# A token-mixer and MLP block with its mixers laid out in three stages: inputs, gates as Strassen sets, one output projection

## The chip, the core and the metric

The kernel runs on one core of a Trainium2 chip. Its time is the device time of one execution, in microseconds (us). The engines that matter are TensorE (PE, matrix products, with a queue of its own for loading weights, PEld), VectorE (DVE), ScalarE (ACT) and GpSimd (POOL). SyncE (SP) does nothing but issue the loads of weights; POOL issues most of the other DMAs. Matrices wait in the on-chip memory SBUF, products are summed in the banks of PSUM, and what does not fit is put in DRAM.

## The reference

One block works on 528 tokens (16 meta tokens and 512 of the sequence) of 2,048 channels, in float32. The first half is two token mixers with three gates, the second a squared-ReLU MLP.

```python
u = rmsnorm(h, norm1_g)                              # 528 x 2048
v_pool, v_lru, v_gelu, g_pool, g_lru = split(u @ w_in)   # five parts of 2048 columns
pool_out = pool_mixer(v_pool)      # causal window means over 2, 4, 8, 16 tokens, then a 512x512 map per group
xc = causal_depthwise_conv(v_lru)  # 4 taps
r, i = sigmoid(xc @ gate_a_w + gate_a_b), sigmoid(xc @ gate_x_w + gate_x_b)   # 8 heads of 256 channels
log_a = -8 * r * softplus(-lam);  a = exp(log_a);  bt = sqrt(-expm1(2 * log_a)) * i * xc
h_t = a_t * h_(t-1) + bt_t         # a scan over the tokens
lru_out = h_t * gelu(v_gelu)
merged = sigmoid(g_pool) * pool_out + sigmoid(g_lru) * lru_out
h = h + merged @ w_out             # 2048 x 2048
h = h + square(relu(rmsnorm(h, norm2_g) @ w1)) @ w2      # 2048 -> 8192 -> 2048
out = rmsnorm(h, final_g)          # the meta tokens are dropped
```

The three gates (g_lru, v_gelu, g_pool) and everything behind them are needed for the 512 tokens alone; v_lru and v_pool are needed for all 528, since the convolution, the scan and the windows look back.

## The kernel before

**Products.** Channels lie on the 128 partitions, tokens along the free axis; a matrix of 2,048 channels is 16 chunks. A weight chunk of 128 x 1024 is loaded from DRAM (SP's queue, 512 KB) and split in two: ACT copies it, rounded, to `whi` (L118), and DVE subtracts that from the chunk into `wlo` (L119). Data is split in the same way. Each product is then three matmuls, whi·xhi, whi·xlo and wlo·xhi (`mm3`, L353 and L635). `Weights` holds four raw chunks and four split ones and splits two ahead of the one in use: `W.next()` hands out a chunk, `W.advance()` asks for the splits of the next. So ACT and DVE split weights all the way through, in between the rest of their work. The order of an engine's instructions is set when the program is built: a scheduler interleaves the instructions of neighbouring steps, and each engine then works strictly through its row.

**Mixers (L308 to L606).** Four quarters of four chunks each. The list `jobs` gives their order: `VL` (a chunk of v_lru: 96 matmuls of 264 columns, then the convolution and the split of its result), `GA` (one LRU head: 48 matmuls of 264 columns, then tanh, reciprocal, sqrt and the scan), `GE`, `GL`, `GP` (one chunk of one gate: 48 matmuls of 512 columns), `VP` (v_pool, 96 matmuls of 264 columns, then window sums on POOL), `PW` (pool map), `WO` (a quarter of the output projection: for each of the 16 output chunks, 12 matmuls of 512 columns over the quarter's four merged chunks, added on DVE to the residual stream `ht`, L560). The first job, `V2`, makes two chunks of v_lru at once while x arrives. The operands x are split without the norm's factor; each evacuation from PSUM multiplies by `rstd` on DVE (`evac_full` L378, `evac` L383). `norm1` (job `N1`) makes `rstd` and stands between `GP` 0 and `GP` 1.

**MLP up (W1).** 32 Strassen sets. A set takes a 2 x 2 block problem (two output chunks by two token halves of 256, over two halves of the channels) and does it with seven products instead of eight: the operands `x11`, `t1`, `t2`, `x21`, `t3`, `x22`, `t4` are sums and differences of the four quarters of x. Each product is 8 chunks of 3 matmuls of 256 columns, 168 matmuls a set (`strassen`, L647; `mm3` L638). The weights' own sums are made on DVE (L107). `finish_h` (squares), `pre_scale`, `forms` (L272: residual times gain and a scale, L278, then the operands and their splits, L284 and L285) and the chain that makes `rho` (L616 to L633) prepare the operands while the last quarter of `WO` runs and behind it. Results of W1 are squared and put in DRAM (`y_sp`).

**MLP down (W2).** 38 steps of Strassen sets over a window of eight `slots` that POOL loads from DRAM, with sums added to `h_sp` in DRAM by DMA; then a last small product and the final norm.

## Time and profile before

| | |
|---|---|
| Times of three runs | 2546.42, 2546.8 and 2571.56 us; median 2546.8 us |
| Profiled execution | 2548.32 us, of which 2546.5 us lie between its first and last instruction (the span) |
| PE busy | 2472.1 us, 97% of the span |
| DVE busy | 1790.6 us, 70% |
| ACT busy | 1051.7 us, 41% |
| POOL busy | 255.0 us, 10% |
| Data read and written in DRAM | 280.85 MB and 54.13 MB |
| Mean granted clock of PE | 0.987 |

In time, the mixers reach to about 1196 us, then come W1 (to about 1859 us), W2 (to about 2460 us) and the tail. The chain of waits follows the work that ended last back to the start, each piece with its start and its length in us; where PE is named all along, PE is what the time goes by. The windows give each engine's busy time in a stretch, with the number of its instructions in brackets, the mean granted clock of PE as a part of full speed, the busy share of the DMA engines and the GB/s that they moved.

### The profile page before, as it was taken

The numbers are of one execution on the slowest core, as the hardware profiler recorded it, in microseconds if no ns is written. First come the engines' busy times: TensorE is split into PE (matmuls) and PEld (weight loads), VectorE is DVE, ScalarE is ACT, GpSimd is POOL, SyncE is SP. The second block draws the span as 40 slices with busy tenths as digits, with TensorE's granted clock in tenths as the row PEclk, the third lists the DMA queues.
The fourth block names the chain that finished last, engine by engine and source line by source line (L and its number), as shares of the span: only waits on it lengthen the run. The fifth ranks groups of instructions, "written<-read, shape, count | busy, mean of one in ns | idle before, by whom it ended". The sixth has DMA issues, their size and how long they took to land.

```text
span 2546.5 us, 41799 instructions
## 1 busy us (share of the span) xinstructions
PE 2472.1 (97%) x17558; PEld 2309.1 (91%) x17558; DVE 1790.6 (70%) x2120; ACT 1051.7 (41%) x1360; POOL 255.0 (10%) x258
## 2 busy tenths in 40 slices
PE   8999999999999999998599999999989999999997
PEld 7889898988889898986599999999979999999996
DVE  8834565445834456338988988988868888878778
ACT  5522233222422234224444444444545454545446
POOL 2100001100202002113100000000010000000010
PEclk9999999999999999999799999999989999999999
DMA  5233333332333323333354554555476665666553
GB/s 194 92 99 91 92 91 92 91 100 91 91 96 92 94 75 108 91 100 99 103 158 154 154 173 151 156 172 151 137 239 168 184 178 174 182 183 186 154 161 105
DMA packets 96604, 337.69 MB, mean 133 GB/s; under 512 B 10720, under 2 KB 18016, under 8 KB 96416
## 3 DMA queue, kind: packets, MB, share of 16 engines
q1 hardware_dynamic: 77648, 251.82, 32.9%
q0 software_dynamic: 18624, 83.11, 10.6%
q8 instruction: 137, 2.24, 0.4%
q14 instruction: 51, 0.42, 0.0%
q10 hardware_dynamic: 144, 0.10, 0.0%
HBM read 280.85 MB, written 54.13 MB: 132 GB/s over the span
## 4 chain that ended last, share of the span: by engine, by line
PE 90%; DVE 6%; issue 1%; DMA 1%; ACT 1%; POOL 0%; SPq 0%; DVEq 0%; ACTq 0%
PE ps_A L638 13%; PE ps_Ab L638 13%; PE ps_vp L357 7%; PE ps_gl L357 7%; PE ps_vl L357 7%; PE ps_B L638 7%; PE ps_gp L357 7%; PE ps_ge L357 7%; PE ps_Bb L638 6%; PE ps_wo L357 6%; PE ps_C L638 3%; PE ps_Cb L638 3%; PE ps_pw L357 2%; PE ga L357 2%; DVE wlo L119 1%
## 5 line engine op out<-in xcount | busy, mean ns | idle before, releaser
L118 ACT ACTIVATE whi<-raw 128x1024 fp32r<-128x1024 f32 (+5 forms) x423 | 428.4, 1015 | 803.1 <-issue 189.8
L119 DVE TENSOR_TENSOR wlo<-raw,whi 128x1024 fp32r<-128x1024 f32 (+5 forms) x423 | 510.2, 1208 | 221.1 <-ACT whi L118 216.2
L638 PE MATMUL ps_Ab<-slot,whi 128*128 128x256 f32 x1984 | 361.0, 283 | 8.4 <-ACT whi L118 3.0
L118 ACT ACTIVATE whi<-sum 128x1024 fp32r<-128x1024 f32 (+7 forms) x210 | 205.6, 979 | 343.8 <-DVE sum L107 165.9
L638 PEld LDWEIGHTS ps_Ab<-slot,whi 128*128 128x128 f32 x1984 | 307.0, 192 | 12.1 <-ACT whi L118 3.8
L638 PE MATMUL ps_Ab<-slot,wlo 128*128 128x256 f32 x992 | 280.3, 283 | 1.3 <-DVE wlo L119 1.2
L119 DVE TENSOR_TENSOR wlo<-sum,whi 128x1024 fp32r<-128x1024 f32 (+7 forms) x210 | 234.8, 1118 | 53.5 <-ACT whi L118 49.4
L638 PEld LDWEIGHTS ps_Ab<-slot,wlo 128*128 128x128 f32 x992 | 188.1, 190 | 2.4 <-DVE wlo L119 2.4
L638 PE MATMUL ps_Bb<-slot,whi 128*128 128x256 f32 x992 | 180.2, 282 | 1.6 <-ACT whi L118 1.6
L107 DVE TENSOR_TENSOR sum<-sum,raw 128x1024 f32<-128x1024 f32 (+7 forms) x140 | 156.5, 1118 | 4.7 <-DMA raw<-w 0.6
L638 PEld LDWEIGHTS ps_Bb<-slot,whi 128*128 128x128 f32 x992 | 152.9, 191 | 2.3 <-ACT whi L118 2.2
L638 PE MATMUL ps_Bb<-slot,wlo 128*128 128x256 f32 x496 | 139.7, 282 | 0.0
L357 PE MATMUL ps_vl<-uh,whi 128*128 128x264 f32 x512 | 106.2, 289 | 7.4 <-ACT whi L118 7.0
L357 PE MATMUL ps_vl<-ul,whi 128*128 128x264 f32 x512 | 105.4, 288 | 0.0
L357 PE MATMUL ps_vl<-uh,wlo 128*128 128x264 f32 x512 | 105.2, 287 | 0.0
L357 PE MATMUL ps_vp<-ul,whi 128*128 128x264 f32 x512 | 104.5, 285 | 0.0
L357 PE MATMUL ps_vp<-uh,wlo 128*128 128x264 f32 x512 | 104.3, 285 | 0.0
L357 PE MATMUL ps_vp<-uh,whi 128*128 128x264 f32 x512 | 104.2, 285 | 0.0
L357 PE MATMUL ps_ge<-ul,whi 128*128 128x512 f32 x256 | 101.2, 395 | 0.0
L357 PE MATMUL ps_gl<-ul,whi 128*128 128x512 f32 x256 | 101.2, 395 | 0.0
L357 PE MATMUL ps_gp<-ul,whi 128*128 128x512 f32 x256 | 101.2, 395 | 0.0
L357 PE MATMUL ps_gp<-uh,wlo 128*128 128x512 f32 x256 | 100.7, 393 | 0.0
(630 smaller groups left out, 6829.3 us busy)
## 6 DMA issues: line engine op xcount, KB each, us to landing
raw<-w SPq DMA_DIRECT2D x168, 512.0 KB, 4.2
raw<-w_in SPq DMA_DIRECT2D x159, 512.0 KB, 3.7
...
slot<-ysp POOLq DMA_DIRECT2D x31, 896.0 KB, 6.3
...
```

What stands on the lines that cost most here:

```text
L107: nc.vector.tensor_tensor(self.raw[o], self.raw[x], self.raw[y], op=ALU.add)
L118: nc.scalar.activation(hi[:, s], raw[:, s], AF.Copy)
L119: nc.vector.tensor_tensor(lo[:, s], raw[:, s], hi[:, s].bitcast(F32), op=ALU.subtract)
L357: PE.matmul(o, a, r, start=first and i == 0, stop=last and i == 2)
L638: PE.matmul(o, a, b, start=first and i == 0, stop=last and i == 2, skip_group_check=True)
```

## The change

The mixers are taken apart into three stages.

**Stage 1, inputs.** Only `VL`, `GA`, `VP`, `PW` and a new job `F` run, in a new written-out order. After `N1` a job `VR` makes chunks 0 and 1 of v_pool and, chunk by chunk ahead of its products, makes the operands of x anew with the norm's factor in them (`rescale_x`: DVE, ACT, DVE). From then on evacuations are plain copies on ACT. The chunks 0, 1 and 2 of v_lru, whose products were made with the old operands, still get the factor on DVE; their convolutions stand behind the rescaling. `F` makes Strassen operands of x for one pair of chunks: `t1` stays in SBUF, `t2`, `t3`, `t4` are put in DRAM (`f_sp`) and fetched at the stage's end (`fill`). Results of the scans and of the pool maps are put in DRAM (`lr_sp`, `pl_sp`). `F` also reads x from DRAM again, since the residual in SBUF gives up its place.

**Stage 2, gates.** For each of eight pairs of chunks, three Strassen sets (`gl`, `ge`, `gp`) of 168 matmuls of 256 columns. The elementwise work is done on tiles of 1,024 columns; the merged pair is split in two parts and put in DRAM (`m_sp`).

**Stage 3, output projection.** All merged chunks are in SBUF, and each output chunk sums over all 16 in PSUM (192 x 4 = 768 matmuls of 512 columns as before, without sums in `ht`): six output chunks at once for pairs 0 to 2, then pairs 3 to 6 one output chunk after another, and pair 7 in four quarters. Operands of W1 are made pair by pair meanwhile; four of the seven are put in DRAM (`g_sp`) and fetched as the merged chunks come free. The first W1 set begins with the first seven chunks of three products, and the last pair's operands are made behind that (`head`); `rho` is made in `middle`.

SBUF is laid out by hand in two large tiles, `a1` and `a2`, which the operands of all stages share. W1, W2 and the tail keep their work; their slots now lie in `a1` and `a2`, and x comes with its tokens ordered by halves. The new weight arrays `woa`, `wob`, `woc` are `w_out` in another order.

```diff
-    jobs = []
-    for q in range(4):
...
+    jobs = "V2_0 VL_2 N1_0 VR_0 GA_0 VL_3 VP_2 GA_1 VP_3 VL_4 PW_0 VL_5 F_0 VP_4 GA_2 VP_5 F_1 VL_6 VP_6 F_2 VL_7"
+    jobs += " VP_7 GA_3 F_3 VL_8 PW_1 VL_9 F_4 VP_8 GA_4 VP_9 VL_10 F_5 VP_10 VL_11 F_6 VP_11 GA_5 VL_12 PW_2 F_7"
+    jobs += " VL_13 VP_12 GA_6 VP_13 VP_14 VL_14 VP_15 VL_15 PW_3 GA_7"
...
+    for c in range(8):
+        for seg in (GL, GE, GP):
+            W.strassen(*(in_chunks(seg, c + 8 * n)[h] for n in range(2) for h in range(2)))
+    for k in range(KD):
+        W.chunk(woa_d[k])
...
+        def rescale_x(k):
+            x = tmp(f"rx{k}")[:, :T]
+            V.scalar_tensor_tensor(x, ht[:, k], pv("g1", k), scale, op0=ALU.mult, op1=ALU.mult)
+            S.activation(ux(k, 0), blocks(x), AF.Copy)
+            V.tensor_tensor(ux(k, 1), blocks(x), ux(k, 0).bitcast(F32), op=ALU.subtract)
...
-        def evac(t, name):
-            z = tmp(name)[:, :SEQ]
-            V.tensor_tensor(z, t, rstd[:, META:], op=ALU.mult)
-            return z
...
+        def evac(t, out, scaled=True):
+            for s, o in ((slice(0, MH), out[:, :META]), (slice(MH, TH), out[:, META:])):
+                if scaled:
+                    S.activation(blocks(o), t[:, :, s], AF.Copy)
+                else:
+                    V.tensor_tensor(blocks(o), t[:, :, s], blocks(scale)[:, :, s], op=ALU.mult)
...
+        def job_VR(c):
+            nonlocal a2
+            ts = in_proj("ps_vr", 2, rescale_x)
+            x_stage.close()
+            pool = ends.enter_context(tc.tile_pool(name="a2", bufs=1, reuse_waits="tile"))
+            a2 = pool.tile([P, 42 * HS], F32R, name="a2")
+            pend[0][1]()
+            pend[1][1]()
+            pend[2][0]()
+            pend[2][1]()
+            for j in range(2):
+                evac_VP(c + j, ts[j])
...
+        def job_F(k):
+            a, b, t = (tmp(f"f{x}{k}")[:, :SEQ] for x in "abt")
+            for x, kk in ((a, k), (b, k + 8)):
+                G.dma_start(blocks(x), blocks(xt_d[:, kk])[:, :, MH:])
+                V.scalar_tensor_tensor(blocks(x), blocks(x), pv("g1", kk), blocks(scale)[:, :, MH:],
+                                       op0=ALU.mult, op1=ALU.mult)
+            (x11, x12), (x21, x22), (t1, t2) = ((x[:, :HS], x[:, HS:]) for x in (a, b, t))
+            V.tensor_tensor(t1, x11, x12, op=ALU.subtract)
+            V.scalar_tensor_tensor(t2, x22, -1.0, t1, op0=ALU.mult, op1=ALU.subtract)
+            t3, t4 = x12, x21
+            V.tensor_tensor(t3, x22, x12, op=ALU.subtract)
+            V.scalar_tensor_tensor(t4, t2, -1.0, x21, op0=ALU.mult, op1=ALU.subtract)
+            put_hl(t1, *place(4)[k])
+            for r, x in (("t2", t2), ("t3", t3), ("t4", t4)):
+                spill(tmp(f"f{r}{k}")[:, :SEQ], x, f_sp[r], k)
...
+            if (kind, i) == ("VL", 15):
+                fill(1, f_sp["t2"], 8)
+            elif (kind, i) == ("PW", 3):
+                fill(5, f_sp["t3"], 8)
+        fill(6, f_sp["t4"], 8)
...
+        if head is not None:
+            first = [(o, W.next(), r) for o, r in ((A, "x11"), (C, "x21"), (B, "t1"))]
+            for o, w, r in first:
+                tiles(o, w, operand(r), range(7), True)
+            head()
+            for o, w, r in first:
+                tiles(o, w, operand(r), range(7, 8), True)
+            after("x11")
+            after("t1")
...
+            middle()
+            after("x21")
...
+        for c in range(8):
+            lm, pl = (gp.tile([P, 2 * SEQ], F32, tag=x, name=f"{x}{c}") for x in ("lm", "pl"))
+            G.dma_start(lm, lr_sp[c].rearrange("p a s -> p (a s)"))
+            G.dma_start(pl, pl_sp[c].rearrange("p a s -> p (a s)"))
+            def gate(seg):
+                z = gp.tile([P, 2 * SEQ], F32, tag="z", name=f"z{seg}{c}", bufs=2)
+                strassen(f"{seg}{c}", X.get, put_plain(z))
+                return z
+            z = gate("gl")
+            S.activation(z, z, AF.Sigmoid)
+            V.tensor_tensor(lm, lm, z, op=ALU.mult)
+            z = gate("ge")
+            w = gp.tile([P, 2 * SEQ], F32, tag="w", name=f"w{c}")
+            S.activation(w, z, AF.Square)
+            V.scalar_tensor_tensor(w, w, 1.0 / 0.044715, z, op0=ALU.add, op1=ALU.mult)
+            S.activation(w, w, AF.Sigmoid, scale=1.5957691216057308 * 0.044715)
+            V.tensor_tensor(z, z, w, op=ALU.mult)
+            V.tensor_tensor(lm, lm, z, op=ALU.mult)
+            z = gate("gp")
+            S.activation(z, z, AF.Sigmoid)
+            V.tensor_tensor(z, z, pl, op=ALU.mult)
+            V.tensor_tensor(lm, lm, z, op=ALU.add)
+            w = gp.tile([P, 2 * SEQ], F32, tag="w", name=f"mh{c}")
+            S.activation(w.bitcast(F32R), lm, AF.Copy)
+            V.tensor_tensor(lm.bitcast(F32R), lm, w, op=ALU.subtract)
+            G.dma_start(m_sp[c][:, : 2 * SEQ], w)
+            G.dma_start(m_sp[c][:, 2 * SEQ :], lm)
...
+    for i in range(8):
+        G.dma_start(merged(i), m_sp[i].bitcast(F32R).rearrange("p (a s) -> p a s", a=4))
...
+    def forms(p, h, u):
+        for a in range(2):
+            V.scalar_tensor_tensor(u[:, a], h[:, a], pv("g2", p + 8 * a), s2, op0=ALU.mult, op1=ALU.mult)
+        t = wo.tile([P, SEQ], F32, tag="t", name=f"t12_{p}")
+        x11, x12, x21, x22 = (u[:, a, b * HS : (b + 1) * HS] for a in range(2) for b in range(2))
+        t1, t2 = t[:, :HS], t[:, HS:]
+        put_hl(x11, *X["x11"][p])
+        put_hl(x21, *X["x21"][p])
+        V.tensor_tensor(t1, x11, x12, op=ALU.subtract)
+        put_hl(t1, *X["t1"][p])
+        V.scalar_tensor_tensor(t2, x22, -1.0, t1, op0=ALU.mult, op1=ALU.subtract)
...
+    ts = [bank("wo", j, SEQ) for j in range(6)]
+    hs = [load_x(p) for p in range(2)]
+    for ch in range(KD):
+        hi, lo = W.next()
+        wo_products(ts, hi, lo, ch, 0)
+        W.advance()
...
+            if (p, a) == (3, 0):
+                pre_scale(2)
+                pair_done(0, hs[0], u=us[0])
+                pair_done(1, hs[1], u=scaled(1))
+                pair_done(2, load_x(2), ts[4:])
+                h = load_x(3)
+        pair_done(p, h, ts3)
...
+    for q in range(4):
+        hi, lo = W.next()
+        for k in range(4):
+            wo_products(ts7, hi, lo, 4 * q + k, 2 * k * P)
+        W.advance()
+        fill(q, g_sp[("t2", "t3", "x22", "t4")[q]], 7)
+    W.ready(W.used + 3)
+    def head():
+        finish_h(7, h7, ts7)
+        u = scaled(7)
+        second = forms(7, h7, u)
+        x = wo.tile([P, 2, SEQ], F32, tag="h", name="sq7", bufs=2)
+        second()
+        square_h(7, h7, x)
...
+        t = bank("r", "", SEQ)
+        PE.matmul(t, ones, ssq, start=True, stop=True, skip_group_check=True)
...
+        strassen(j, X.get, put, **(dict(head=head, middle=middle) if j == 0 else {}))
```

The next pieces show rows of an engine's order, each with its line, its operation, the tile it writes, the tiles it reads and the size; "x4" stands for four such in a row.

On DVE, at the end of the first norm, before. `rstd` is the norm's factor, `v` an evacuated chunk of v_lru, `xc` its convolution.

```order
L264 TENSOR_TENSOR n1b<-n1b,n1a 128x528
L265 TENSOR_SCALAR n1b<-n1b 128x528
L266 TENSOR_TENSOR rstd<-rstd,n1b 128x528
L378 TENSOR_TENSOR v_568<-ps_vl_157,rstd 128x528
L378 TENSOR_TENSOR v_580<-ps_vl_158,rstd 128x528
L421 TENSOR_SCALAR xc_571<-v_568,par 128x528
L421 TENSOR_SCALAR xc_583<-v_580,par 128x528
L423 SCALAR_TENSOR_TENSOR xc_571<-v_568,par,xc_571 128x528
```

The same place after; `scale` is the norm's factor, `rx` the scaled x, `a` the large tile with the operands.

```order
L314 TENSOR_TENSOR n1b<-n1b,n1a 128x528
L315 TENSOR_SCALAR n1b<-n1b 128x528
L316 TENSOR_TENSOR scale<-scale,n1b 128x528
L411 TENSOR_TENSOR v_632<-ps_v_198,scale 128x16
L411 TENSOR_TENSOR v_632<-ps_v_198,scale 128x512
L411 TENSOR_TENSOR v_636<-ps_v_199,scale 128x16
L411 TENSOR_TENSOR v_636<-ps_v_199,scale 128x512
L361 SCALAR_TENSOR_TENSOR rx_661<-ht,par,scale 128x528
L361 SCALAR_TENSOR_TENSOR rx_677<-ht,par,scale 128x528
L361 SCALAR_TENSOR_TENSOR rx_693<-ht,par,scale 128x528
L363 TENSOR_TENSOR a_84<-rx_661,a_84 128x2x264
```

The evacuations of the two first chunks stand there as before; behind them now comes the rescaling in groups of three, and the convolutions have moved behind all of it.

On PE at the same place, before. `psn` is the norm's sum over channels, `ps_gp` a gate's chunk.

```order
L357 MATMUL ps_gp_465<-ul,whi_415 128x512
L357 MATMUL ps_gp_465<-uh,wlo_416 128x512
L348 MATMUL psn_529<-ssq_71,ones 128x264
L348 MATMUL psn_529<-ssq_72,ones 128x264
L348 MATMUL psn_533<-ssq_71,ones 128x264
L348 MATMUL psn_533<-ssq_72,ones 128x264
L357 MATMUL ps_gp_594<-uh,whi_490 128x512
L357 MATMUL ps_gp_594<-ul,whi_490 128x512
```

After, with `ps_vl_0` chunk 2 of v_lru and `ps_vr` the two chunks of v_pool:

```order
L332 MATMUL ps_vl_0_506<-a_84,whi_456 128x264 x4
L332 MATMUL ps_vl_0_506<-a_84,wlo_457 128x264 x2
L380 MATMUL psn_617<-ssq_196,ones 128x264
L380 MATMUL psn_617<-ssq_197,ones 128x264
L380 MATMUL psn_621<-ssq_196,ones 128x264
L380 MATMUL psn_621<-ssq_197,ones 128x264
L332 MATMUL ps_vr_659<-a_84,whi_555 128x264 x2
L332 MATMUL ps_vr_660<-a_84,whi_609 128x264 x2
L332 MATMUL ps_vr_659<-a_84,whi_555 128x264 x2
L332 MATMUL ps_vr_659<-a_84,wlo_556 128x264 x2
```

Behind the norm's four matmuls stood a gate's chunk with the old operands; now there stand products that read the rescaled ones.

On DVE in the gates, before: the evacuations of a gate's chunk (L383), what is done with it (L473 to L487) and the splits of weights (L119) in turn.

```order
L119 TENSOR_TENSOR wlo_1378<-raw_1241,whi_1377 128x1024
L383 TENSOR_TENSOR gz_1343<-ps_ge_1282,rstd 128x512
L119 TENSOR_TENSOR wlo_1408<-raw_1271,whi_1407 128x1024
L473 TENSOR_SCALAR gw_1345<-gw_1345 128x512
L477 TENSOR_TENSOR xc_977<-xc_977,gz_1343 128x512
L119 TENSOR_TENSOR wlo_1443<-raw_1311,whi_1442 128x1024
L383 TENSOR_TENSOR glz_1413<-ps_gl_1352,rstd 128x512
L119 TENSOR_TENSOR wlo_1473<-raw_1341,whi_1472 128x1024
L487 TENSOR_TENSOR xc_571<-xc_571,glz_1413 128x512
L119 TENSOR_TENSOR wlo_1508<-raw_1381,whi_1507 128x1024
```

After, across the end of a `gp` set and the start of the next `gl` set (L664: an evacuation of 256 columns; L699, L700, L703: the set's elementwise work; `sum`, `w`: sums of weights at L109; L118: splits of weights).

```order
L664 TENSOR_TENSOR zgp_5933<-ps_Bgp_5935,u_gp_5938 128x256
L118 TENSOR_TENSOR wlo_6202<-sum_6150,whi_6201 128x1024
L109 TENSOR_TENSOR sum_6150<-sum_6150,raw_6061 128x1024
L118 TENSOR_TENSOR wlo_6231<-raw_6061,whi_6230 128x1024
L109 TENSOR_TENSOR sum_6385<-w_6094,raw_6264 128x1024
L699 TENSOR_TENSOR zgp_5933<-zgp_5933,pl_5476 128x1024
L118 TENSOR_TENSOR wlo_6261<-w_5865,whi_6260 128x1024
L700 TENSOR_TENSOR lm_5475<-lm_5475,zgp_5933 128x1024
L118 TENSOR_TENSOR wlo_6293<-sum_6150,whi_6292 128x1024
L109 TENSOR_TENSOR w_6094<-w_6094,raw_6092 128x1024
L703 TENSOR_TENSOR lm_5475<-lm_5475,mh_6159 128x1024
L118 TENSOR_TENSOR wlo_6324<-raw_6029,whi_6323 128x1024
```

The elementwise rows are twice as wide, and between them stand the splits and sums for the next set's products.

More of the change, by code (lines that the diff above doesn't have):

```diff
@@ L129, in prefetch @@
             tag = self.loads[self.loaded][1]
-            if not self.free[tag] or (tag != "raw" and self.sums is None):
+            if not self.free[tag]:
                 return
@@ L134, in ready @@
     def ready(self, splits):
-        while self.split < min(splits, len(self.ops), self.limit):
+        while self.split < min(splits, len(self.ops)):
             self._split()
@@ new lines, in build, with mm3s @@
+    lr_sp, pl_sp = ([dram.tile([P, 2, SEQ], F32, name=f"{x}{c}") for c in range(8)] for x in ("lr", "pl"))
+    m_sp = [dram.tile([P, 4 * SEQ], F32, name=f"msp{c}") for c in range(8)]
+    v_sp = dram.tile([P, SEQ], F32, name="vsp")
+    f_sp = {r: dram.tile([P, 2, 8 * HS], F32, name=f"fsp_{r}") for r in ("t2", "t3", "t4")}
+    g_sp = {r: dram.tile([P, 2, 8 * HS], F32, name=f"gsp_{r}") for r in ("t2", "t3", "x22", "t4")}
+    def mm3s(ps, w, mh, ml, first, last):
+        wh, wl = w
+        for i, (a, b) in enumerate(((wh, mh), (wh, ml), (wl, mh))):
+            for o, r in zip(ps, b):
+                PE.matmul(o, a, r, start=first and i == 0, stop=last and i == 2)
@@ L377, in evac_full @@
[L377 to L402 removed]
+            rms_scale(scale, ssq[0], a[:, :T], b[:, :T])
@@ L594, in pre_scale @@
[L594 to L604 removed]
+            hi, lo = dsp_at(c)
@@ L679, in strassen @@
         W.advance()
-        if not late:
-            product_c()
+        if head is None:
+            product(C, "x21", True)
+            after("x21")
+            W.advance()
+        else:
+            middle()
+            after("x21")
         product(A, "t3", False)
```

664 lines of the change are left out of this document (317 added, 347 removed).

## The prediction

> **What bounds the kernel now.** The page's first part comes first, then the chain's shares:
>
> ```profile
> span 2546.5 us, 41799 instructions
> ...
> PE 2472.1 (97%) x17558; PEld 2309.1 (91%) x17558; DVE 1790.6 (70%) x2120; ACT 1051.7 (41%) x1360; POOL 255.0 (10%) x258
> ...
> PE 90%; DVE 6%; issue 1%; DMA 1%; ACT 1%; POOL 0%; SPq 0%; DVEq 0%; ACTq 0%
> ```
>
> PE bounds nearly everything; DVE holds 6% of the chain. Where, the windows by stage show (window, length; busy us of PE, PEld, DVE, ACT, POOL; clock; DMA share; GB/s):
>
> ```profile
> 59.50:1151.30 1091.80, 1090.46 (x6238) 957.02 (x6238) 567.66 (x631) 329.63 (x384) 124.73 (x88) 1.00 0.31 93
> 1151.30:1195.70 44.40, 41.10 (x164) 32.04 (x163) 32.80 (x39) 19.71 (x27) 17.13 (x14) 0.92 0.32 102
> 1195.70:1249.60 53.90, 22.87 (x100) 18.23 (x99) 51.78 (x67) 20.98 (x34) 14.66 (x9) 0.69 0.19 65
> 1249.60:1303.90 54.30, 50.24 (x419) 49.56 (x419) 46.11 (x55) 24.69 (x30) 2.73 (x5) 0.96 0.51 166
> 1303.90:1858.60 554.70, 554.70 (x4897) 554.70 (x4896) 491.33 (x616) 265.98 (x320) 33.36 (x62) 1.00 0.52 160
> ...
> 1949.40:2424.30 474.90, 474.90 (x4035) 474.90 (x4034) 385.47 (x361) 239.15 (x288) 32.96 (x46) 1.00 0.61 176
> ```
>
> The mixers lose 1.3 us of PE in 1092, W1 and W2 nothing. The hole is 1195.7 to 1249.6, between mixers and W1: DVE busy 51.8 of 53.9 us, PE 22.9, its clock down to 0.69. The chain of waits gives the rates (start, length, count) and shows the hole from inside:
>
> ```profile
> 139.02 44.48 PE ps_gl L357 x192
> ...
> 458.68 46.96 PE ps_vp L357 x384
> ...
> 868.08 44.68 PE ps_wo L357 x192
> ...
> 1151.49 11.17 PE ps_wo L357 x48
> ...
> 1165.95 2.08 PE ps_s L598 x2
> ...
> 1177.09 3.69 DVE ht L278 x4
> ...
> 1236.14 3.28 DVE r L621
> ...
> 1246.36 4.58 PE ps_B L638 x22
> ```
>
> ```profile
> 1322.90 5.44 PE ps_A L638 x48
> ...
> 1341.94 5.44 PE ps_A L638 x48
> ```
>
> ```profile
> 1966.52 5.65 PE ps_Ab L638 x48
> ...
> 1986.30 5.65 PE ps_Ab L638 x48
> ```
>
> A matmul of 512 columns takes 44.48/192 = 231.7 ns (232.7 in `WO`), one of 264 46.96/384 = 122.3. A Strassen set of 168 matmuls of 256 columns takes 19.04 us in W1 (113.3 ns each) and 19.78 in W2 (117.7): two rates for one shape, both at a granted clock of 1.00.
>
> **Gates as Strassen sets.** Removed: 3 gates x 16 chunks x 48 = 2304 matmuls of 512 columns, 2304 x 231.7 = 533.8 us. Added: 24 x 168 = 4032 of 256 columns: 456.8 us at W1's rate, 474.6 at W2's. By columns alone (7/8) it would be 467. I take W2's: three of the seven operands (`x11`, `x21`, `x22`) lie in blocks 264 apart, as the operands of the 264-wide matmuls do, whose 122.3 ns are 118.6 for 256 columns. Gain 59 (to 77).
>
> The Trainium skill ("TensorE: Matmul & The Clock Gate", Back-to-back issue gap) gives a sustained spacing of about 81 ns at N=128 and 131 ns at N=512, by which narrower matmuls pay a large fixed part; between these figures 256 columns would take some 98 ns, an estimate, and the sets would cost 4032 x 98 - 2304 x 131 = 93 us more. The trace differs: 231.7 ns for 512 and 113.3 for 256 leave no such fixed part, so the measured rates stand, and the rule gets no chance of its own.
>
> Can DVE and ACT keep up? Their rows in W1, and its busy time in 500 us:
>
> ```profile
> L119 DVE TENSOR_TENSOR wlo<-raw,whi 128x1024 fp32r<-128x1024 f32 x87 | 106.4, 1222 | 20.9 <-ACT whi L118 18.0
> ...
> L107 DVE TENSOR_TENSOR sum<-sum,raw 128x1024 f32<-128x1024 f32 x58 | 71.1, 1226 | 2.0
> ...
> L734 DVE TENSOR_TENSOR y<-ps_A,q 128x256 f32<-128x256 f32 x29 | 12.3, 425 | 14.8 <-PE ps_A L638 14.8
> ```
>
> ```profile
> L749 ACT ACTIVATE y<-y 128x1024 f32<-128x1024 f32 x29 | 30.9, 1064 | 30.7 <-DVE y L740 30.6
> ...
> L667 ACT ACTIVATE p<-ps_A 128x256 f32<-128x256 f32 x29 | 10.5, 363 | 0.0
> ```
>
> ```profile
> 1300.00:1800.00 500.00, 500.00 (x4415) 500.00 (x4414) 446.60 (x552) 240.69 (x288) 27.98 (x52) 1.00 0.53 159
> ```
>
> A gate set needs on DVE 7 splits and 4 sums of 1.22 us and 3 evacuations of 0.425, 14.7 us, and one (`gl`) or three (`ge`, `gp`) elementwise operations of 1.22. Three sets: 44.1 + 8.5 = 52.6 us beside 59.3 of PE, 89%; in W1 it is 446.6/500, also 89%, and PE loses nothing there. The order of DVE puts each elementwise row between splits, not all at the set's end. I cost it at nothing; without that cover it is the rival below. Weights are 2 MB a set as in W1, where the DMA engines are busy 53%; `lr_sp`, `pl_sp` and `m_sp` add 2 MB per three sets, a third more, 71% at most. The 512-wide evacuations (L383) that leave stood beside PE and free nothing.
>
> **Between mixers and W1.** The last quarter of `WO` starts at 1151.5 and has 192 x 232.7 ns = 44.7 us, so PE could begin W1 at 1196.2. W1 ends at 1858.6 and has 32 x 19.04 = 609.3 us, so it began, in effect, at 1249.3: 53 us lost, held by DVE's forms (L278) and the chain of `r` (L621). After, seven of eight pairs' forms stand beside PE's own products: a pair has 96 matmuls of 512 columns, 22 us, and needs on DVE six operations of 512 columns (3.69/4 = 0.92 us each at L278, where POOL works too), eleven of 256 (0.425) and four splits of weights, 15 us. What remains is pair 7. `head` needs four operations of 512 columns and four of 256 before its three products can end, 5.4 us, covered by 63 matmuls (7.1). The norm's sum stands on PE ahead of `t2`: it waits for some seven more operations of 256 columns (3.0), a square (1.06) and two additions (1.4), 5.5 us with 1.7 and nine matmuls (1.0) as cover, 3; its matmul takes 2 (`ps_s`), and a late fill of `t4` 2 to 3. Loss after 8, bounds 3 and 25; gain 45 (28 to 50).
>
> **The start.** `norm1` in before, on DVE, and PE beside it:
>
> ```profile
> 47.73 0.77 DVE L349 COPY ssq<-psn 128x264 f32<-128x264 f32 x2
> ...
> 51.02 3.45 DVE L262 RECIPROCAL rstd<-n1b 128x528 f32<-128x528 f32 x1 [2.02 <-ACT n1b L261]
> 54.39 1.16 DVE L119 TENSOR_TENSOR wlo<-raw,whi 128x1024 fp32r<-128x1024 f32 x1
> ...
> 57.41 0.71 DVE L266 TENSOR_TENSOR rstd<-rstd,n1b 128x528 f32<-128x528 f32 x1
> 58.15 1.32 DVE L378 TENSOR_TENSOR v<-ps_vl,rstd 128x528 f32<-128x528 f32 x2
> ```
>
> ```profile
> 34.58 11.12 PE ps_gp L357 x48
> ...
> 47.48 3.51 PE ps_gp L357 x16
> ...
> 59.01 11.96 PE ps_vl L357 x96
> ```
>
> ```profile
> L423 DVE SCALAR_TENSOR_TENSOR xc<-v,par,xc 128x528 f32<-128x528 f32 x33 | 25.3, 766 | 0.6
> ...
> L462 DVE TENSOR_TENSOR gs<-gs,gs 128x528 f32<-128x528 f32 x12 | 8.4, 702 | 0.0
> ...
> L421 DVE TENSOR_SCALAR xc<-v,par 128x528 f32<-128x528 f32 x11 | 6.1, 555 | 0.3
> ```
>
> Now `GP` 1 hides the norm. After, `VL` 2 (96 x 122.3 = 11.7) takes `GP` 0's place, and the norm's matmuls end about 48.1; nothing follows that could run. The chain from 47.73 to 58.15 without the split in it is 9.3 us; two evacuations (1.5), the first scaling (0.77) and its copy on ACT (0.65, between its rows of 256 and 1024) follow. PE stands still from 48.1 to 60.7: 12.6 us. Then DVE paces `VR`: 16 x (0.77 + 0.70) and two splits, 26 us against 23.5 of PE, 2 more. `GA` 0 waits behind all of it for two convolutions (2 x (0.56 + 3 x 0.77) = 5.7), the third chunk's evacuation (0.8) and the splits, less one product: 6.5. Sum 21; before waits 0.4 here (`GP` 1 ends at 47.48 + 11.12 = 58.6, `VL` begins at 59.0). Loss 20.5, bounds 12.6 and 26. The granted clock fell to 0.69 in the window at 1195.7; a dip here is absorbed where DVE paces PE. The Trainium skill (the same page, The HAM clock gate) states half speed for some 3.4 us after such idle time, by which this sum would grow by at most 1.7, an estimate.
>
> Then evacuations leave DVE for ACT: each `VL` and `VP` frees 0.7 us of a DVE busy 568 of 1092 us. No gain, as PE didn't wait.
>
> **The rest of stage 1 and its end.** DVE's longest operation and POOL's largest load in before:
>
> ```profile
> L453 DVE RECIPROCAL y<-y 128x528 f32<-128x528 f32 x12 | 40.5, 3419 | 0.0
> ...
> slot<-ysp POOLq DMA_DIRECT2D x31, 896.0 KB, 6.3
> ```
>
> Eight heads now fall in 466 us of PE's work (32 x 11.74 + 8 x 5.9 + 16 x 2.8) instead of 1092, and DVE has in it about 350 us: 16 convolutions with splits (57), 16 pools (22), 8 heads of 14 (two reciprocals of 3.42 and ten shorter operations), 80 splits of weights (98), `F` (42) and the rescaling (24). The nearest row is the mixers' own, 1.3 us lost at 52% DVE; against it stands that the last head's 14 us of DVE fall together with the first gate set's splits. POOL issues the parking DMAs, and POOL's additions for the windows wait behind them. I take 10, nearer to the row than to the 14 a head (112) that would be the upper end; for the range 0 to 40.
>
> Gates to `WO`: six of the eight merged pairs can be fetched while the last set runs, each 1 MB at the slot's rate 7 us; the last is needed 14 x 18 x 0.232 = 58 us into `WO`. Nothing. `WO` itself keeps its 768 matmuls at 232.7; DVE additions to `ht` fall from 64 to 16, hidden before as after.
>
> **W1, W2, tail.** Same work; nothing, if each keeps its rate.
>
> **The sum.** -59 - 45 + 20.5 + 10 = -73.5, say -74. Span 2546.5 - 74 = 2472.5; the profiled execution lies 1.8 above its span (2548.32 and 2546.5), 2474.3, and 1.5 above the median of the runs (2546.8): about 2473 us.
>
> **The rivals.**
>
> *The other rate.* What chooses 113.3 or 117.7 the trace doesn't tell. Gates at W1's rate: 18 less, 2455. W2's long window at it too (4035 x 4.4 ns): another 18, 2437. W1 at W2's (5376 x 4.4 = 24): 2497; that the slowest run lies 25 above the median speaks for this happening at all.
>
> *Stage 1 waits more*, POOL's queue or DVE behind the heads: 40 instead of 10, 2503.
>
> *The set's end uncovered (slower).* If DVE waited in its row for ACT at the end of each gate set, with no split ahead, the whole chain would show: `gl` a copy, a sigmoid and a multiplication, 0.36 + 1.06 + 1.22 = 2.6; `ge` 0.36 + 2 x 1.06 + 3 x 1.22 = 6.1, `gp` the same with two copies and three operations. 14.9 a pair, 8 pairs: 119 us, and 2473 + 119 = 2592. For it: at 89% DVE has 6.7 us to spare in three sets. Against it: W1's window, as full and without loss. At 74/119, 62% of the chain bare, the change is worth nothing; at 84% it is 1% slower.
>
> *It doesn't do what it says*: the hole between mixers and W1 stays, because `head` and `rho` end as late as now: -74 + 45 = -29, 2518.
>
> **How the numbers follow.** About 1% is what a measurement tells from no change: 2521 and 2572. The forecast, with small errors, 0.42; a faster rate in gates or W2, 0.22; W1 at the slower rate, 0.12; stage 1, 0.12; the hole stays, 0.07; the set's end bare, 0.05. Faster by over 1% are the first four nearly whole and part of the fifth: 0.86; within 1%: the rest of it, the stage 1 case at its worst, the rate and stage 1 together: 0.09; slower 0.05. The range takes in both faster rates and stage 1 with 2 us over it: 2437 to 2505; left out is 0.07 + 0.05 and some joint cases.
>
> **What would show it.** Gates: 24 sets 19.0 or 19.8 us apart with no DVE or ACT between in the chain of waits. The start: PE idle about 48 to 61, and a second wait ahead of `ga`. Between `WO` and W1's second set: under 10 us lost. W1 and W2: 19.04 and 19.78 a set. Wrong it would be if the chain showed `wlo` or `lm` in the gates, or if a rate were a third one.

## The result and the profile after

The changed kernel takes 2487.05 us (median of four runs, 2461.09 to 2504.17) where the kernel before takes 2546.61: a ratio of 0.971, 95% interval 0.962 to 0.980. The forecast was 2473, 2437 to 2505. The profiled execution is the fastest of the four, 2461.09 us. For most of its length W1 or W2 runs at one of two rates, 113.3 or 117.7 ns a matmul, and which one differs between executions, so below stages are compared, not totals.

The first part of the page after, and the shares of its chain of waits:

```profile
span 2459.0 us, 46248 instructions
...
PE 2381.9 (97%) x19286; PEld 2327.9 (95%) x19286; DVE 1981.6 (81%) x2371; ACT 1195.1 (49%) x1633; POOL 290.2 (12%) x377
...
PE 23%; DVE 2%; DMA 1%; issue 1%; ACT 0%; DVEq 0%; ACTq 0%
```

PE still bounds the kernel; its busy time fell by 90.2 us while DVE's grew by 191. The chain can be followed only back to W2's start this time (its shares add to 27%), so the windows have to carry the reading (columns as before: window, length; busy us of PE, PEld, DVE, ACT, POOL; clock; DMA share; GB/s):

```profile
46.00:100.00 54.00, 40.67 (x292) 39.28 (x291) 52.55 (x74) 27.98 (x43) 7.24 (x4) 0.84 0.20 65
100.00:509.00 409.00, 400.63 (x3073) 391.19 (x3073) 280.86 (x344) 172.04 (x263) 119.72 (x123) 0.99 0.42 139
509.00:560.00 51.00, 43.06 (x353) 42.66 (x352) 40.80 (x40) 23.55 (x31) 5.81 (x8) 0.90 0.52 180
560.00:985.00 425.00, 425.00 (x3682) 425.00 (x3681) 363.32 (x357) 223.19 (x277) 18.74 (x35) 1.00 0.45 153
985.00:1160.00 175.00, 175.00 (x773) 144.58 (x772) 101.51 (x159) 63.52 (x95) 35.81 (x54) 1.00 0.63 212
1160.00:1228.00 68.00, 56.06 (x419) 52.95 (x418) 54.32 (x74) 27.74 (x39) 7.59 (x13) 0.92 0.67 238
1228.00:1790.00 562.00, 562.00 (x4961) 562.00 (x4960) 498.74 (x624) 269.88 (x325) 33.91 (x63) 1.00 0.50 163
```

Three places lose PE time: the start (40.67 of 54), the first gate set (43.06 of 51) and the start of W1 (56.06 of 68); 8.4 us more are spread over the 409 us of stage 1. Gates behind the first set and `WO` lose nothing; the gates take 425/3682 = 115.4 ns a matmul, between the two rates considered.

PE's timeline gives the borders and the waits of the start and of W1 (start, length, what; idle before and its releaser in brackets):

```profile
45.81 0.83 PE L380 MATMUL psn<-ssq,ones 128*128 128x264 f32 x3
57.94 2.11 PE L332 MATMUL ps_vr<-a,whi 128*128 128x264 f32 x6 [11.30 <-DVE rx L361]
```

```profile
1160.23 0.40 PE L337 MATMUL ps_A<-a,whi 128*128 128x256 f32 x2
...
1172.62 2.08 PE L853 MATMUL ps_r<-ssq,ones 128*128 128x512 f32 x2 [3.75 <-DVE ssq L742]
...
1182.01 0.47 PE L337 MATMUL ps_B<-a,whi 128*128 128x256 f32 x2 [4.00 <-DMA a<-gsp_x]
```

```profile
1790.15 0.28 PE L337 MATMUL ps_A<-a,wlo 128*128 128x256 f32 x1
```

W1 runs from 1160.2 to 1790.3, 630 us, of which 609.3 are its 32 sets at 19.04: 20.7 lost, where 53 were lost before. (Some expectations below have 640.3 and 31 here: they were measured to the first product of W2 that reads from the large tile, some 10 us behind W1's end. That product marks the end in every run compared there, so their differences hold.)

Where the 87.5 us between the two spans (2546.5 and 2459.0) come from:

| Stage | before | after | change, us | forecast |
|---|---|---|---|---|
| Gates (24 x 19.40 of PE work) | 533.8 | 465.6 | -68.2 | -59 |
| Start, to the first `GA` product | | | +15.7 | +20.5 |
| First gate set, its wait and the lower clock behind it (509.1 to 985.2 less 465.6) | 0 | 10.4 | +10.4 | +10, with the next row |
| Rest of stage 1, what is left over | | | +9.7 | |
| `WO` (985.2 to 1160.2) | 178.7 | 175.0 | -3.7 | 0 |
| Mixers to W1, loss | 53 | 20.7 | -32.3 | -45 |
| W2, at 113.3 instead of 117.7 | 639.7 | 620.0 | -19.7 | 0 |
| Tail | | | +0.6 | 0 |

### The profile page after: what moved, and what is told of

Its sections match the earlier page's. It is cut to its first block, busy times and chain, and to the rows that moved or that the text cites. A ratio compares the mean times of both kernels' runs of the same rounds, so it can differ in the third digit from the quotient of the medians.

```text
span 2459.0 us, 46248 instructions
## 1 busy us (share of the span) xinstructions
PE 2381.9 (97%) x19286; PEld 2327.9 (95%) x19286; DVE 1981.6 (81%) x2371; ACT 1195.1 (49%) x1633; POOL 290.2 (12%) x377
## 5 line engine op out<-in xcount | busy, mean ns | idle before, releaser
L117 ACT ACTIVATE whi<-raw 128x1024 fp32r<-128x1024 f32 (+6 forms) x403 | 402.8, 1003 | 401.5 <-issue 92.7
L118 DVE TENSOR_TENSOR wlo<-raw,whi 128x1024 fp32r<-128x1024 f32 (+6 forms) x403 | 468.8, 1166 | 138.7 <-ACT whi L117 134.9
L117 ACT ACTIVATE whi<-sum 128x1024 fp32r<-128x1024 f32 (+5 forms) x282 | 282.3, 1001 | 467.5 <-DVE sum L109 225.2
L118 DVE TENSOR_TENSOR wlo<-sum,whi 128x1024 fp32r<-128x1024 f32 (+5 forms) x282 | 322.1, 1142 | 86.9 <-ACT whi L117 83.6
L337 PE MATMUL ps_A<-a,whi 128*128 128x256 f32 x2048 | 356.3, 277 | 2.1 <-ACT whi L117 1.6
L337 PEld LDWEIGHTS ps_A<-a,whi 128*128 128x128 f32 x2048 | 310.2, 189 | 4.0 <-ACT whi L117 2.0
L337 PE MATMUL ps_Ab<-a,whi 128*128 128x256 f32 x1728 | 305.7, 277 | 1.3 <-ACT u_b L636 0.8
L337 PE MATMUL ps_A<-a,wlo 128*128 128x256 f32 x1024 | 283.5, 277 | 0.6 <-DVE wlo L118 0.6
L337 PEld LDWEIGHTS ps_Ab<-a,whi 128*128 128x128 f32 x1728 | 261.6, 189 | 2.4 <-ACT u_b L636 1.2
L337 PE MATMUL ps_Ab<-a,wlo 128*128 128x256 f32 x864 | 239.4, 277 | 0.0
L109 DVE TENSOR_TENSOR sum<-sum,raw 128x1024 f32<-128x1024 f32 (+7 forms) x188 | 215.2, 1145 | 5.6
L109 DVE TENSOR_TENSOR sum<-w,raw 128x1024 f32<-128x1024 f32 (+7 forms) x94 | 107.2, 1140 | 40.7 <-DMA raw<-w 37.2
```

The costliest lines, as they stand in the source:

```text
L109: nc.vector.tensor_tensor(self.raw[o], self.raw[x], self.raw[y], op=ALU.add)
L117: nc.scalar.activation(hi[:, s], raw[:, s], AF.Copy)
L118: nc.vector.tensor_tensor(lo[:, s], raw[:, s], hi[:, s].bitcast(F32), op=ALU.subtract)
L337: PE.matmul(o, a, b, start=first and i == 0, stop=last and i == 2, skip_group_check=True)
```

## The experiments

The theory: the gates gain by columns and by where the operands lie; part of the gain is given back at three places where DVE's row or a DMA holds PE. The rivals were that the set's rate has another cause, that DVE has no room left in the gates, and that each of the three places has a wait behind the wait.

### The operands' places in the gates

The gates' products of `x11`, `x21` and `x22` took 2.84 us, the other four 2.72. The first kernel takes those three operands from places 256 apart that hold other data of the same kind; the count of matmuls stays.

```diff
-        X[r] = [tuple(a1[:, i * PL + (8 * j + k) * TH + MH : i * PL + (8 * j + k + 1) * TH] for j in range(2))
-                for k in range(8)]
+        X[r] = place(i)
```

> The changed kernel, with the gates' operands x11, x21 and x22 read at a spacing of 256 instead of 264 columns (so these three are not the right numbers: the gates' values are others, the work is the same). In the changed kernel their products take 2.84 us and the other four 2.72. Theory (the place in SBUF makes them slow): all seven take 2.72, a set 19.04 instead of 19.40, the eight pairs 24 x 0.36 = 8.6 us less. Rival (it is the place in the set, or what DVE and ACT do beside them): they stay at 2.84.

The second has 64 bytes more of constants a partition, so that all operands in the two large tiles begin 64 bytes further on; the weights lie ahead of the constants and stay. (The places modulo 256 bytes in the expectation are a count of the layout; no trace prints an address, and what is shown is the shift of 64 bytes.)

```diff
+    V.memset(const.tile([P, 16], F32, name="shift64"), 0.0)
```

> The changed kernel with 64 bytes more of constants, which moves the two operand tiles by 64 bytes against the weights: operands spaced 256 columns begin at 0 instead of 192 modulo 256 bytes. Reading x11, x21 and x22 at a spacing of 256 brought their products from 2.84 to 2.72 us; in the 264 spacing the chunk that begins at 0 took 357 ns for its three matmuls, those at 192 340 to 351. Theory (where an operand begins modulo 256 bytes counts, and 192 is the fast place): products spaced 256 take 2.8 to 2.86 in gates, W1 and W2, 50 to 70 us more in all. Rival (the spacing counts, a change of place from chunk to chunk): 2.72 in gates and W1 as now.

The same windows, of PE alone, in gates and in W1 (window, length, PE busy and its matmuls, clock, DMA share, GB/s): the changed kernel, the operands 256 apart, and 64 bytes on.

```profile
560.00:960.00 400.00, 400.00 (x3467) 1.00 0.44 146
1240.00:1760.00 520.00, 520.00 (x4590) 1.00 0.49 160
```

```profile
560.00:960.00 400.00, 400.00 (x3532) 1.00 0.44 147
1240.00:1760.00 520.00, 520.00 (x4591) 1.00 0.48 159
```

```profile
560.00:960.00 400.00, 400.00 (x3356) 1.00 0.42 142
1240.00:1760.00 520.00, 516.92 (x4291) 1.00 0.46 151
```

In the gates 115.4 ns a matmul become 113.3 in the first and 119.2 in the second; in W1 113.3 stay in the first and become 120.5 in the second. The first kernel took 2472.88 us (W2 at 117.7), its gates 468.1 instead of 476.1. The second took 2544.31, 83 more than the profiled execution after: 15 in gates, 36 in W1, 30 in W2 (which at 117.7 would have lost 20 by itself) and 3 in `WO`. The first came out as its theory said; the second went the theory's way and somewhat beyond its figures (2.88 us a product, where 2.86 was the most). So what a 256-column matmul takes depends on where its moving operand starts. In the second, even the pattern inside a product moved on: the eight chunks of an operand 264 apart took 351, 357, 359, 358, 357, 358, 353 and 347 ns for three matmuls, and 359, 358, 357, 358, 353, 347, 351 and 357 after the shift. From one chunk to the next the place moves by 264 x 4 = 1056 bytes, 32 more than four times 256, so 64 bytes are two such steps, and by two steps the pattern moved. It isn't a rule for every shape: `WO`'s operands of 512 columns took 175.0 us at their place and 178.1 with it shifted, 2% against 6.

### Room on DVE in the gates

Two more operations of 1024 columns on DVE at the end of each gate set, which change no value:

```diff
             z = gate("gl")
             S.activation(z, z, AF.Sigmoid)
+            V.tensor_tensor(z, z, z, op=ALU.max)
+            V.tensor_tensor(z, z, z, op=ALU.max)
             V.tensor_tensor(lm, lm, z, op=ALU.mult)
```

> The changed kernel with two more DVE operations of 1024 columns (1.22 us each) behind each gate's sigmoid, so in the chain at the end of every gate set. DVE then needs 52.6 + 7.3 = 59.9 us per three sets, PE 58.2 at the measured 19.40 a set. The prediction's rule (covered until DVE is full): the gates take 8 x 1.7 = 14 us more than the 476 of the changed kernel, 485 to 500. The prediction's slower rival (what stands at the set's end is bare): 24 x 2.44 = 59 more, 525 to 545. No effect: 476 to 479.

PE's waits in that kernel from 520 to 992 us (what waited for what: us in total, times, longest):

```profile
PE ps_Cgl L337 <- DVE wlo L118: 8.3, 1, 8.3
PE ps_Agl L337 <- DVE zgl L668: 2.9, 7, 0.7
```

The gates took 481.6 us instead of 476.1, between "no effect" (476 to 479) and the rule's 485 to 500. The 48 operations are 59 us of DVE, and 5.5 reach the end; the wait of 8.3 in the first set is there without them too (7.9). So the rival in which the chain at the end of a set stands bare falls: even lengthened it is nearly all covered by the splits. The rule counted DVE as more than full (59.9 of 58.2 us a pair); in the trace it was busy for 380.7 of the 400 us from 560 on, where it had been 345.3, so the room was larger than the forecast counted. (The whole run took 2511.48 us; W1 ran at 117.7 in it.)

### The start and the end of stage 1

One kernel has the norm's matmuls and DVE chain in the middle of `VL` 2 instead of behind it:

```diff
+                last = norm1() if h and name == "ps_vl2_" else None
+                with tc.issue_after(last.ins) if last is not None else ExitStack():
...
-            norm1()
```

> The changed kernel with the first norm's four matmuls in the middle of v_lru's chunk 2 instead of behind it, and the second half of that chunk queued behind them. Theory (the 11.7 us in which PE stands still are the norm's chain with nothing beside it): half of the chunk, 5.9 us, now lies beside the chain; DVE gets one weight split into the chain that waits for the chunk's end, so PE stands still for 7 to 9 us and VR begins at 53 to 55 us instead of 57.9. Rival (what is waited for is DVE's rescaling, whatever the norm does): VR begins at 57 to 58.

```profile
55.51 2.11 PE L332 MATMUL ps_vr<-a,whi 128*128 128x264 f32 x6 [9.08 <-DVE rx L361]
```

`VR` begins at 55.5, later than the 53 to 55 expected, and earlier than in any profile with the old order (57.4 to 58.7): PE is out of products before DVE is through. Whether the gain arrives isn't shown: the first gate set begins at 507.5, and in the profiles whose stage 1 is that of the changed kernel it begins between 507.3 and 509.8. (2481.44 us; W2 at 117.7.)

The other puts `GA` 7 ahead of `PW` 3, so that head 7's DVE chain would be done when the first gate set needs its splits:

```diff
-    jobs += " VL_13 VP_12 GA_6 VP_13 VP_14 VL_14 VP_15 VL_15 PW_3 GA_7"
+    jobs += " VL_13 VP_12 GA_6 VP_13 VL_14 VP_14 VL_15 VP_15 GA_7 PW_3"
...
-            if (kind, i) == ("VL", 15):
+            if (kind, i) == ("VP", 15):
```

> The changed kernel with the end of stage 1 in another order: GA 7 ahead of PW 3 instead of behind it, v_lru's last two chunks earlier. In the changed kernel PE waits 8.1 us in the first gate set for a weight split that stands on DVE behind the last head's work. Theory (the head's 14 us of DVE fall on the first set): with 11 us of PW 3 between, that wait goes, and from the first GA to the end of the gates it takes 7 to 9 us less (before: 85.8 to 985.1, 899.3 us). Rival (DVE is late anyway there, since its work is the same): the wait moves ahead of PW 3 or stays within the first set, and the stretch changes by less than 3 us. Rates of 113.3 or 117.7 ns a matmul may differ from run to run, so the stretch up to the first set's end is compared as well.

DVE's row at the end of stage 1 in the changed kernel shows what it was meant to move (two reciprocals of one head ahead of the first split of the set):

```profile
510.79 6.75 DVE L496 RECIPROCAL y<-y 128x528 f32<-128x528 f32 x2
...
521.71 1.21 DVE L118 TENSOR_TENSOR wlo<-raw,whi 128x1024 fp32r<-128x1024 f32 x1
```

PE's waits from 430 to 560 us with `GA` 7 ahead:

```profile
PE ps_Bgl L337 <- DVE wlo L118: 4.6, 1, 4.6
...
PE ps_pw L332 <- ACT po L545: 2.3, 1, 2.3
PE ps_Cgl L337 <- DVE wlo L118: 1.0, 1, 1.0
```

The theory fell here. From the first `GA` product to the end of the gates it took 903.8 us, against 899.4 (897.1 in a second profile of the changed kernel). The waits for `wlo` in the first set went from 7.9 to 5.6, not to nothing, since the reciprocals now lie at 504 to 512; and `PW` 3, whose operations off PE had been hidden, waits itself, 2.8 us. The gates begin 6 us later; what the rest of that is, with the last `VL` and `VP` jobs in another order too, wasn't tried. (2490.61 us; W2 at 117.7.)

### Mixers to W1

In the changed kernel, waits between 1160 and 1228 us:

```profile
ACT whi L117 <- issue: 10.7, 2, 8.5
...
ACT slot L893 <- DMA slot<-ysp: 9.1, 1, 9.1
DVE wlo L118 <- ACT whi L117: 8.9, 3, 7.5
...
PE ps_B L337 <- DMA a<-gsp_x: 4.0, 1, 4.0
...
PE ps_r L853 <- DVE ssq L742: 3.7, 1, 3.7
```

and its DMA issues from 1135 to 1226 (operation, count, KB each, median us from issue to landing):

```profile
a<-gsp_t POOLq DMA_DIRECT2D x3, 1792.0 KB, 13.4
raw<-w SPq DMA_DIRECT2D x10, 512.0 KB, 5.5
a<-gsp_x POOLq DMA_DIRECT2D x1, 1792.0 KB, 12.1
```

Four fills of 1.8 MB fall together with W1's first weights. Also, slot 0's load and split, written for W1's 31st set, stand in the rows of POOL and ACT at 1213 to 1221. Three kernels try the fills, the forms' buffers and the norm's matmul; the slot is moved only in the kernel with all of it. W1's own scatter bounds what can be read: 630.0 us here, and 630.4, 630.4 and 634.7 in three kernels (norm early, operands 256 apart, `GA` 7 ahead) that change nothing in it.

*The fills cut*, chunks 0 to 5 first and chunk 6 behind, so that the last chunk alone waits for pair 7:

```diff
-        fill(q, g_sp[("t2", "t3", "x22", "t4")[q]], 7)
+        fill(q, g_sp[("t2", "t3", "x22", "t4")[q]], 6)
...
+    for q in range(4):
+        t = a1[:, q * PL : q * PL + 16 * HS].rearrange("p (a n) -> p a n", a=2)[:, :, 6 * HS : 7 * HS]
+        G.dma_start(t, g_sp[("t2", "t3", "x22", "t4")[q]][:, :, 6 * HS : 7 * HS].bitcast(F32R))
```

> The changed kernel with each of the four fills of W1's operands from DRAM cut in two: pairs 0 to 5 at once as the place comes free, pair 6 in a small load behind all. In the changed kernel all four fills stand on POOL behind pair 6's stores and land 12 to 18 us after WO, PE loses 31 us up to the second set, among it 4.3 us for x22, and waits for splits whose raw weights come late. Theory (the fills wait for pair 6's stores, then crowd out the weights): three of four fills run beside pair 7's products, and from the end of WO to the end of W1 it takes 12 to 20 us less than 640.3. Rival (the loss is pair 7's own forms, the norm's sum and the clock that falls with them): less than 6 us change.

```profile
PE ps_A L337 <- ACT p L614: 5.4, 1, 5.4
PE ps_r L856 <- DVE ssq L742: 3.0, 1, 3.0
PE ps_A L337 <- DVE wlo L118: 2.3, 1, 2.3
```

No gain: 640.6 us against 640.3. The wait for a fill is gone from PE's list, and in its place stands one for ACT's `p` (5.4), ahead of which ACT was idle for 9.4 us without a releaser that the profile shows. That wait isn't the edit's alone: the changed kernel's second profile, below, has 3.9 for `p` beside 2.1 for the fill. The theory fell. (2462.32 us.)

*The fills of one chunk instead of seven*, which takes the DMA traffic away; six of the seven chunks then hold other data:

```diff
-        fill(q, g_sp[("t2", "t3", "x22", "t4")[q]], 7)
+        fill(q, g_sp[("t2", "t3", "x22", "t4")[q]], 1)
```

> The changed kernel, with the four fills at the end of WO fetching one chunk of eight instead of seven (W1's operands t2, t3, x22, t4 of pairs 1 to 6 are then not the right numbers; 1 MB moved there instead of 7.3). Cutting the fills in two changed nothing (640.6 us from the end of WO to the end of W1, against 640.3), and there a norm operation on DVE waited 6.3 us for the store of pair 7's residual, which crossed the fills. Theory (what PE loses there is the DMA engines' crowding by 7.3 MB, whoever waits for it: x22's fill, raw weights, the store): the loss of 31 us falls to 10 to 18. Rival (forms, norm's sum and the fallen clock): it stays above 26.

```profile
1160.00:1228.00 68.00, 60.43 (x471) 57.77 (x470) 63.08 (x83) 32.31 (x44) 8.05 (x14) 0.92 0.51 170
```

W1 lost 14.6 us (1160.8 to 1784.7) instead of 20.7: the fills' traffic is 6 of the 21, between what theory and rival said. PE's waits are now for DVE's `ssq` (3.8) and `wlo` (1.7) and ACT's `a` (1.4). (2478.38 us; W2 at 117.7.)

*The fills cut, three buffers for the forms, the norm's matmul behind `t2`'s product:*

```diff
-    v2 = wo.tile([P, SEQ], F32, name="v2")
...
-        t = bank("s", "", SEQ)
+        t, v2 = bank("s", "", SEQ), wo.tile([P, SEQ], F32, tag="f", name="v2", bufs=3)
...
-                    f = wo.tile([P, SEQ], F32, tag="f", name=f"{r}_{p}", bufs=2)
+                    f = wo.tile([P, SEQ], F32, tag="f", name=f"{r}_{p}", bufs=3)
...
-        PE.matmul(t, ones, ssq, start=True, stop=True, skip_group_check=True)
+        with tc.issue_after(t2.ins):
+            PE.matmul(t, ones, ssq, start=True, stop=True, skip_group_check=True)
```

> The changed kernel with three edits at the end of WO: the fills cut in two as before, the parked forms in three buffers instead of two (the pre-norm's spare tile becomes one of them), and the second norm's sum queued on PE behind the product of t2 instead of ahead of it. Theory (pair 6's forms end at 1161 because a form's buffer waits for its store, and PE waits 4 us for the sum of squares with a product at hand): the fills issue some 5 us earlier, the wait for the sum goes: 8 to 15 us of the 31 come back. Rival (the last to come is DMA traffic that only moves): under 5 us, and the wait turns up at x22, t4 or a weight split.

```profile
PE ps_A L337 <- DMA a<-gsp_t: 7.3, 1, 7.3
PE ps_A L337 <- ACT p L616: 4.4, 2, 3.9
```

The rival held in size: W1 took 629.6 us. The wait for `ssq` is gone from this list, and `t2`'s last piece, now behind the other fills in POOL's queue, holds PE for 7.3. (2479.93 us; W2 at 117.7.)

### All of it together

The norm early; the fills of `t2` and `t3` whole and ahead of `x22`'s, `t4`'s behind the residual store of pair 7; three buffers; the norm's matmul behind `t2`; slot 0's load behind the 30th set's store. The new lines beside those shown above (`rest(q)` is the loop's body from the kernel with the fills cut, for one operand, and hands back the DMA):

```diff
-        fill(q, g_sp[("t2", "t3", "x22", "t4")[q]], 7)
+        if q == 3:
+            break
+        with tc.issue_after(piece.ins) if q > 1 else ExitStack():
+            fill(q, g_sp[("t2", "t3", "x22", "t4")[q]], 6)
+        if q == 1:
+            rest(0)
+        if q:
+            piece = rest(q)
...
-        finish_h(7, h7, ts7)
+        stored = finish_h(7, h7, ts7)
+        with tc.issue_after(stored.ins):
+            fill(3, g_sp["t4"], 7)
...
-            load_slot(0, nc.gpsimd)
+            with tc.issue_after(stored.ins):
+                load_slot(0, nc.gpsimd)
```

> The changed kernel with the early norm and with the end of WO in another order: t2's and t3's fills whole ahead of x22's, t4's behind the store of pair 7's residual, parked forms in three buffers, the norm's sum behind t2's product, and the first W2 slot loaded behind W1's 30th set instead of in its second (where ACT waited 8 to 9 us for it). In the three runs before, each wait at the end of WO that was taken away was followed by another (x22's fill, t2's last piece, the store of pair 7's residual, the slot). Theory (together they are what PE loses there, 20 us): W1, from its first matmul to its last, takes 612 to 620 us instead of 630, VR begins at 55 to 56, and the fastest run is 2443 to 2451 us. Rival (each hides the next one still): over 625, and the fastest run 2456 or more.

PE's waits from 1150 to 1228 us, and the window of W1's start:

```profile
PE ps_A L337 <- ACT p L618: 0.6, 1, 0.6
PE ps_B L337 <- DVE wlo L118: 0.5, 1, 0.5
PE ps_A L337 <- DMA a<-gsp_t: 0.3, 1, 0.3
PE ps_A L337 <- DVE wlo L118: 0.3, 1, 0.3
```

```profile
1160.00:1228.00 68.00, 66.25 (x566) 64.99 (x566) 67.38 (x92) 34.73 (x47) 5.83 (x10) 1.00 0.65 229
```

W1 takes 616.4 us (1159.8 to 1776.2), a loss of 7.1 where 20.7 were. The kernel takes 2452.1 us (median of six, 2446.94 to 2453.73), 0.9646 of the kernel before (0.961 to 0.968): it beats both. W1 and the fastest run are within what was expected; `VR` begins at 56.5, not at 55 to 56. The span of 2450.7 is 8.3 below that of the changed kernel's first profile, in which W1 and W2 ran at 113.3 as they do here. Of the 13.6 us that W1 gains, 5.8 are lost again in W2 (625.9 us, where the first profile had 620.1 at the same rate), 2.3 of them in its first 168 matmuls; the cause wasn't followed up. The rest of the distance between the medians would be the rate: all six runs lie within 7 us, so none of them can have had the slower rate all through W1 or W2, which most runs of the changed kernel seem to have had. Whether the edits or luck brought that is open.

The changed kernel beside it on the same chip:

> The changed kernel as it is, beside the one above on the same chip. Runs between 2460 and 2505 us as before, by the rate of 113.3 or 117.7 ns a matmul that W1 and W2 take in a run.

```profile
560.00:960.00 400.00, 400.00 (x3467) 1.00 0.42 146
1240.00:1760.00 520.00, 520.00 (x4418) 1.00 0.45 153
1900.00:2350.00 450.00, 450.00 (x3824) 1.00 0.61 179
```

2480.95 us (2467.56 to 2505.31), a ratio of 0.9746 (0.970 to 0.979). The profiled execution is the slowest, 2503.5 between first and last instruction, and shows both W1 (520/4418) and W2 (450/3824) at 117.7 ns, with gates at 115.4 as ever. W1 is 25.6 us longer than in the first profile and W2 19.9, and they begin 1.1 earlier: together the 44 between the two spans. What sets the rate stays open. In the kernel before, W2's matmuls changed from 113.3 to 117.7 ns at 1946 us, behind two that start 0.37 us apart, and here W2's did so at 1903 us, behind two that start 0.124 us apart; the granted clock is 1.00 at both rates.

## Why the prediction was right, step by step

**Gates, -59 (to -77): right in kind, 9 too careful.** The 89% of DVE in W1 was a sound measure: PE stands without a gap in 23 of 24 sets, and 59 us more of DVE cost 5.5. The forecast took W2's rate for all seven operands, from the three 264 apart. Those three measured 118.3 ns a matmul, as was read from the 122.3 of the 264-wide ones; the four others ran at 113.3. A matmul of 512 columns takes 227.9 ns in `WO` (175.0/768) and one of 256 about half of that, 113.3: no fixed part per matmul shows. That answers the gap figures of the Trainium skill ("TensorE: Matmul & The Clock Gate", Back-to-back issue gap), by which, as the forecast estimated, the sets would have cost more than the products that they replace.

**The start, +20.5: 15.7.** PE's idle time came out nearly as summed, 11.3 us (the bracket at 57.94) for 12.6. `VR` took 26.1 us for the 26 of the forecast, but by luck: DVE doesn't pace it. Behind its first product no wait of PE is listed in `VR`; what makes it longer than 192 matmuls of 121.8 ns (23.4 us) is mostly PE's clock. `GA` 0's wait was 1.9 us for 6.5. With 0.4 taken off for before, the three make 15.5. The start of `VR` (columns as above), the last operand of `VR` on DVE, and PE's next product behind `VR`:

```profile
57.94:63.20 5.26, 5.20 (x22) 4.89 (x23) 5.26 (x9) 3.21 (x5) 0.00 (x0) 0.51 0.00 0
```

```profile
77.76 0.70 DVE L363 TENSOR_TENSOR a<-rx,a 128x528 fp32r<-128x528 f32 x1
```

```profile
85.78 0.51 PE L332 MATMUL ga<-a,whi 128*128 128x264 f32 x2 [1.71 <-ACT a L468]
```

DVE was through with `VR` at 78.5, PE at 84.1 (85.8 less the 1.7 waited): 5.6 us of products covered the convolutions, where the forecast had counted one product. The clock dipped to 0.51 in the first of these lines: two matmuls of `VR` took 0.44 us until 62.9 and 0.25 from 63.2 on, half speed for some 5 us. The forecast had this dip absorbed beside DVE's pace; it is in fact most of the 2.7 us that `VR` was longer. The Trainium skill ("TensorE: Matmul & The Clock Gate", The HAM clock gate) has some 3.4 us for this; here it was longer.

**The rest of stage 1 and its end, +10 (0 to 40): 20.** The mishap that was named, the last head's DVE chain against the first set's splits, is half of it, a wait of 7.9 us and then a clock of 0.50 from 517 to 526:

```profile
PE ps_Cgl L337 <- DVE wlo L118: 7.9, 1, 7.9
```

The forecast weighed it against "the mixers' own" 1.3 us and settled near the row of the old arrangement, in which no head stood at a border. Other waits of PE, 8.3 us in total with the longest at about 270, 310 and 429, were for ACT (`gs` and `whi`). That ACT, which takes over the evacuations, could be late next was not weighed; whether these are what delays it wasn't tried.

**Mixers to W1, -45 (28 to 50): -32.** This step failed in size: "loss after 8" was 20.7, inside its bounds of 25. The terms it had, `ssq` (3 forecast, 3.7 measured) and a late fill (2 to 3, 4.0 measured), are in PE's waits. What it left out is that the four fills run together and with W1's first weights (6 us, by the kernel with small fills); that the weights then come late to ACT and so to DVE's splits, and that a slot's split moved up into the same row adds to it, is read from the rows and wasn't tried alone. PE's waits in the window add to 11.9 us (68.0 less 56.06), 3.7 of them for weights; the norm's matmul takes 2, and a clock of 0.92 over 68 us is some 5. One or a few of the causes taken away gave 0, 6 and 0.4 us, all of them 13.6, so waits did stand behind waits. The last kernel differs from the one before it by the fills' order and the slot's load (and the early norm, far ahead); which of these two brings most of the 13 us between them isn't shown.

**`WO`, W1, W2, tail: 0.** `WO` came out 3.7 shorter. W1 kept 113.3. W2's step to 113.3 in the profiled execution is the rival "the other rate", in the place in which it was put; that it differs between executions was only hinted at by the slowest run before, and the range held it by that: 2461 to 2504 are one kernel, and a later run took 2505.31.

**The sum.** Without W2's rate the profiled execution would have been 2480.8, 6.5 above the 2474.3 that the forecast had for it (a run took 2481.06, but its stages aren't on record). Better gates (-9), `WO` (-4) and start (-5) stand against a worse transition (+13) and stage 1 (+10): that the figure was nearer than its terms is luck.

**The rivals.** The slower one, 119 us of bare chain, fell. "The hole stays" fell. "Stage 1 waits more" happened by a third: 20 us, where it had 40 and the forecast 10. Of the signs of being wrong, two showed in part: a gate set took 19.40 us, neither 19.0 nor 19.8, since its operands lie at two kinds of places, and `wlo` held PE in the gates, once, in the first set.
